# Two more Strassen blocks per MLP, squares moved to the scalar engine, and one address remainder for the matmul operands: a two-layer decoder trunk on one Trainium2 core

## The chip, the core and the metric

The kernel runs on one core of one Trainium2 chip. A core has four compute engines that run side by side, each with its own queue in program order: TensorE (PE in the profile; its loads of the stationary operand are shown apart as PEld), VectorE (DVE), ScalarE (ACT) and GpSimd (POOL). SyncE (SP) issues nearly all DMAs. The metric is device time of one launch in microseconds (us). Lower is better.

## The reference

A sequence of 256 tokens of width 1024 goes through two layers in float32. Each layer is an attention block and an MLP with squared ReLU:

```
def sqrelu_mlp(x, w1, w2):
    h = jax.nn.relu(x @ w1)
    return (h * h) @ w2

def reference(x, ...):
    h = x
    for layer in range(2):
        hn = rms_norm(h, norm_gain[layer, 0])
        h = h + (stick_breaking_attention(hn, ...) if layer == 0 else nsa_attention(hn, ..., shared))
        h = h + sqrelu_mlp(rms_norm(h, norm_gain[layer, 1]), mlp_w1[layer], mlp_w2[layer])
        if layer == 0:
            shared = nsa_shared_kv(h, kv_norm, ...)
    return rms_norm(h, final_norm)
```

`mlp_w1` is 1024 x 4096 and `mlp_w2` is 4096 x 1024. The change concerns the two MLPs, the transposes that lead into them, and one small product in the second layer's query projection.

## The kernel before

**Products in two parts.** Every large float32 product is made of three fast ones. An operand a is cut into a high part (rounded to the matmul's float32 form, fp32r) and a low part (a minus high). Then a.b is high.high + high.low + low.high. `mm3` issues these three. For weights, the high part is a cast on ACT (`cast`, L356, tile `wh`), the low part a subtraction on DVE (L371, tile `wl`), both from a 128 x 1024 tile `raw` that a DMA fills. There are six buffers each of `raw`, `wh` and `wl`.

**The MLP** (`mlp`, called once per layer) runs over 16 blocks of 256 hidden units. For block c, `first` multiplies the transposed normalised stream `xn` by two column halves of w1, 16 matmuls of 512 columns and 16 of 256 in all, into the PSUM tiles `pu`. ACT copies these to SBUF (`mu`, L630). `square` adds the two halves of `mu` (L645), takes relu and square in one DVE instruction (L646), cuts the result `ms` into `hh` (ACT, L650) and `hl` (DVE, L651), and makes the sums and differences of its 128 x 128 blocks that the second product wants (L659 to L662). `half(c, ., 0)` and `half(c, ., 1)` then multiply by the two halves of w2 into the PSUM tiles `acc`. Block c's `half` stands two blocks later in PE's queue: the loop over c issues `first(c)` and then the halves of block c - 2.

**Plain and fast blocks.** A block's second product is a 2 x 2 product of 128-row blocks (two halves of tokens, two halves of hidden units) with 512 columns of output each. A plain block takes 8 products, so 24 matmuls of 128 x 512 columns. The blocks listed in `FAST` use Strassen's scheme, 7 products and 21 matmuls. They need sums of w2's tiles (`sums`: `ty`, L384, L389, L390), and these sums cut into `th` and `tl` (L356, L397; four buffers each) besides the weights as they are. `FAST` before is blocks 2, 4, 6, 8, 10, 12 in both layers.

**What sets the order.** PE's order is the order of the Python code. The order on ACT, DVE and POOL is set while the program is built, by a planner (`Order`): each small operation is put with a rank and a cost in ns for each engine that may do it, and an engine that is free takes the ready operation of lowest rank. `o.quiet("D", ns)` keeps DVE from work of rank 2 or more for that time. Weights have rank 0.5 when PE needs them next, 2 or 4 when later.

**The start of an MLP.** `xt_turn` transposes the stream on PE (tiles `pt`), and `xt_evac` takes each transposed tile into `xn`: the high part on ACT (L504), the low part on DVE (L505). Half of the tiles is turned before the MLP, half inside it, after `first` of block 0's first half.

**The query projection of layer 1.** `q_proj` makes rotated queries of one of four head groups g: ACT copies to `qu` (L1233), DVE multiplies (`qm`, L1234) and shuffles (`qw`, L1236), then a product by a table (`qw`, L1237) and a sum (`qm`, L1240) that the planner may give to POOL or DVE.

**Addresses.** An SBUF tile's address within a partition is set when the program is built. The tiles `raw`, `wh`, `wl`, `xn`, `oT`, `xk` and `xq` all start at 160 bytes past a multiple of 256. The MLP's own pool starts at byte 156192, so `ms`, `hh`, `hl`, `th` and `tl` start at 32 past a multiple of 256.

Of the kernel before, what the change touches and what calls it, by code (L numbers as in the profile page):

```python
# [8 lines left out]
F32 = mybir.dt.float32  # L9
F32R = mybir.dt.float32r  # L10
BF16 = mybir.dt.bfloat16
AF = mybir.ActivationFunctionType
OP = mybir.AluOpType
AX = mybir.AxisListType

P = 128
D = 1024
# [7 lines left out]
DFF = 4096  # L25
NFC = 16
NGN = 6
FAST = ((2, 4, 6, 8, 10, 12),) * 2
EPS = 1e-5
NEG = -1e30  # L30
GELU_C = 2.0 * 0.7978845608028654
# [127 lines left out]
def act(n, f, more=0):  # L159
    return {"A": (195 + 0.835 * n + more, f, False)}  # L160


def dve(n, f, more=0, port=False):
    return {"D": (150 + 1.045 * n + more, f, port)}
# [7 lines left out]
def hybrid_kernel(ctx, tc, x, xt, eye, gcols, gfin, wqk, wv, wo0, wkv, wvs, wq, wg, wo1, w1, w2, cw1, cw2, cpos, gate_b, consts, out):  # L172
    nc = tc.nc
# [7 lines left out]
    o = Order()  # L181

    def go(gen, rank=1, lag=LAG):
        return Chain(o, gen, rank, o.now + lag)
# [3 lines left out]
    def f32(a):  # L188
        return a.bitcast(F32)

    def slot(i, shape, dt, name):
        return cp.tile(shape, dt, tag=f"e{i}", name=name, bufs=1)
# [4 lines left out]
    def B(i, name, dt=F32):  # L197
        return ps.tile([P, 512], dt, tag=f"b{i}", name=name, bufs=1)
# [7 lines left out]
    def feed(src, n, kind="w", parts=1, cuts=1, own=False, only=None):  # L206
        loads.append((src, n, cuts, own))
        return item(kind, only or n, [len(loads) - 1], parts)
# [14 lines left out]
    def feed_mlp(layer):  # L223
# [6 lines left out]
        def two(c, wide):  # L230
            s = [w2[layer, c][:, h * H:(h + 1) * H] for h in range(2)]
            fast = c in FAST[layer]
            x = feed(s[0], H)
# [180 lines left out]
    def W(i, part=None):  # L414
        if i > ws.cur:
            ws.cur = i
            for q in range(i, min(i + 4, len(items))):
                for c in ws.parts[q] or ():
                    c.hurry(rank_of(q))
        while any(ws.parts[q] is None for q in range(i + 1)):  # L420
            o.run(o.run(o.t))
        for p in range(items[i][3]) if part is None else (part,):
            for q in range(items[i][4] + p + 1):
                c = ws.parts[home[q]][q - items[home[q]][4]]
                if not c.done:
                    c.hurry()
            o.need(ws.parts[i][p])
        return ws.raws[items[i][2][0]] if items[i][0] == "r" else ws.made[i]

    def gone(x):  # L430
        for i in x if isinstance(x, list) else [x]:
            assert ws.gone == i, (ws.gone, i)
            ws.gone += 1
            if items[i][0] == "r":
                used(items[i][2][0])
        now, ws.waiting = ws.waiting, []
        for w in now:
            o.at(o.now, w.finish)
# [15 lines left out]
    def tr(o_, a, i, rate=2.0):  # L454
        nc.tensor.transpose(o_, a, i)  # L455
        o.tick(a.shape[0] / 2.4 * rate + 3)
# [39 lines left out]
    def xt_banks(banks):  # L496
        return [B(banks[b], f"pt{b}").rearrange("p (j q) -> p j q", j=2) for b in range(2)]

    def xt_evac(pt, j, b, half, gi, xt_, rank=0.5):
        k = 4 * half + 2 * b + j  # L500
        g = gc[:, gi * NK + k:gi * NK + k + 1]

        def one():
            yield act(256, lambda: nc.scalar.activation(xt_[0][:, k, :], pt[b][:, j, :], AF.Copy, scale=g), 60)  # L504
            yield dve(256, lambda: nc.vector.scalar_tensor_tensor(  # L505
                xt_[1][:, k, :], pt[b][:, j, :], g, f32(xt_[0][:, k, :]), op0=OP.mult, op1=OP.subtract), 60)
        return go(one(), rank)

    def xt_turn(pt, half, gi, xt_):
        ch = []  # L510
        for b in range(2):
            for j in range(2):
                k = 4 * half + 2 * b + j
                for t in range(T):
                    tr(pt[b][:, j, t * P:(t + 1) * P], hres[t][:, k * P:(k + 1) * P], ident)
            ch += [xt_evac(pt, j, b, half, gi, xt_) for j in range(2)]
        return ch
# [35 lines left out]
    def mlp(layer, gi, x_, ch, pt, rs, pus, accs, extra, mid, order, ends, ap):  # L553

        ws.tp = ap
        mus = slot(1, [P, 2, 2, 512], F32, "mu")
        mu = [mus[:, i] for i in range(2)]
        wa, wb = i_m[layer]
        fast = FAST[layer]
        acc = {}  # L560
# [40 lines left out]
        def begin(c):  # L601
            return ([B(pus[c % 2][f], f"pu{f}") for f in range(2)] if c < 4 else [None, None],
                    (mu[c % 2], ap.tile([P, 9, P], F32, name="ms")), [])
# [30 lines left out]
        def square(c, st):  # L634
            u, s = st[1]
            hh = ap.tile([P, 8 * P], F32R, name="hh", bufs=3)
            hl = ap.tile([P, 8 * P], F32R, name="hl", bufs=3)
            u4 = u.rearrange("p f (a q) -> p f a q", a=2)
            s4 = s[:, 0:4].rearrange("p (f t) q -> p f (t q)", f=2)
            flat = s.rearrange("p b q -> p (b q)")  # L640

            def gen():
                for x in st[2]:
                    yield x
                yield dve(512, lambda: nc.vector.tensor_add(s4, u4[:, :, 0], u4[:, :, 1]), port=True)  # L645
                yield dve(512, lambda: nc.vector.scalar_tensor_tensor(s4, s4, 0.0, s4, op0=OP.max, op1=OP.mult), port=True)  # L646

            def parts(a, b, at):
                q, into = slice(a * P, b * P), slice(at * P, (at + b - a) * P)
                yield act((b - a) * P, lambda: nc.scalar.copy(hh[:, into], flat[:, q]))  # L650
                yield dve((b - a) * P, lambda: nc.vector.tensor_sub(hl[:, into], flat[:, q], f32(hh[:, into])), port=True)  # L651

            def plain(g):
                yield g
                yield from parts(0, 4, 0)

            def mixed(g):
                yield g
                yield dve(256, lambda: nc.vector.tensor_sub(s[:, 4:6], s[:, 2::-2], s[:, 3:0:-2]), port=True)  # L659
                if c in fast:  # L660
                    yield dve(256, lambda: nc.vector.tensor_sub(s[:, 6:8], s[:, 1:5:3], s[:, 3:6:2]), port=True)
                    yield dve(128, lambda: nc.vector.tensor_sub(s[:, 8], s[:, 6], s[:, 0]), port=True)  # L662
                    yield from parts(5, 9, 4)
                else:
                    yield from parts(4, 6, 4)

            g = go(gen(), 0.4)
            at = {a: a for a in range(4)}
            at.update({S3: 4, S1: 5, S4: 6, S2: 7} if c in fast else {E2: 4, S3: 5})
            return hh, hl, (go(plain(g), 0.4), go(mixed(g), 0.41)), at  # L670
# [3 lines left out]
            first(0, st[0], f, 0, NK // 2)  # L674
        gone(wa[0][0])
        o.need(*rs)
        ch.extend(xt_turn(pt, 1, gi, x_))
        st.append(begin(1))
        for f in range(2):
# [315 lines left out]
    def layer1(xk, pt0, ch, ap):  # L995
# [215 lines left out]
        def q_proj(g, b, k0=0, k1=NK):  # L1211
            if k0 == 0:
                qps[g] = B(b, "qp")
            qp = qps[g]
            for k in range(k0, k1):
                w = W(i_q[g][k // 4])
                for j in range(2):
                    c = k % 4 * 256 + j * P
                    o.need(qc[k])
                    mm3(qp[:, j * 256:(j + 1) * 256], cut(w, c, c + P), both(xq, k), j == 0 and k == 0, k == NK - 1)  # L1220
                if k % 4 == 3:
                    gone(i_q[g][k // 4])
            if k1 < NK:
                return

            def gen():
                u = ap.tile([P, 2, T * P], F32, name="qu", bufs=3)
                m = ap.tile([P, 2, T * P], F32, name="qm", bufs=3)
                s = ap.tile([P, 2, T * P], F32, name="qw")
                src = qp.rearrange("p (j q) -> p j q", j=2)  # L1230
                tab = [rbc_[:, i, None, :].to_broadcast([P, 2, T * P]) for i in range(2)]
                yield rbc
                yield [act(512, lambda: nc.scalar.copy(u, src), -35),  # L1233
                       dve(512, lambda: nc.vector.tensor_mul(m, src, tab[0]))]  # L1234
                qu[g] = u
                yield dve(512, lambda: nc.vector.stream_shuffle(s, u, swap), 50)  # L1236
                yield {"G": (1040, lambda: nc.gpsimd.tensor_mul(s, s, tab[1]), True),  # L1237
                       "D": (690, lambda: nc.vector.tensor_mul(s, s, tab[1]), True)}
                yield {"G": (1260, lambda: nc.gpsimd.tensor_add(m, m, s), True),
                       "D": (690, lambda: nc.vector.tensor_add(m, m, s), True)}  # L1240
                qs[g] = m
            qch[g] = go(gen(), 0.8)

        qps, pvs = {}, {}
# [322 lines left out]
        pt = xt_banks((6, 7))  # L1567
# [14 lines left out]
    x1, ch, pt, rs = scoped(layer0, "l0")  # L1582
# [13 lines left out]
    x1, ch, pt, rs = scoped(layer1, "l1", nxt["x"], nxt["pt"], nxt["ch"], bufs=1)  # L1596
# [153 lines left out]
```

## Time and profile before

| | |
|---|---|
| median of 3 runs | 616.29 us (615.42 to 616.64) |
| the profiled execution, own time | 616.42 us |
| its span, first to last instruction | 614.6 us |
| mean granted TensorE clock | 0.997 |
| PE busy | 604.0 us (98%) |
| DVE busy | 507.2 us (83%) |
| ACT busy | 377.1 us (61%) |
| POOL busy | 40.6 us (7%) |

The profiled execution is 0.13 us above the median, and 1.8 us of it lie outside the span. The first MLP runs on PE from about 115 to 291 us of the span, the second from about 431 to 606 us. Busy PE time is a union of matmul records that overlap each other, so it doesn't tell how fast the matmuls follow one another. For that one reads the chain of waits, whose pieces lie end to end: a piece of so many matmuls, divided by their number, is the spacing from one to the next.

### The profile page before, as it was taken

Reading aid. Unit: us, or ns where it says so; the run is one execution under the profiler, and the core shown is the slowest. Engines: PE = TensorE matmul, PEld = TensorE weight load, DVE = VectorE, ACT = ScalarE, POOL = GpSimd, SP = SyncE. Lnnn points to the kernel's source line nnn. Section 1 sums busy time; section 2 is a strip of 40 time slices with the busy share of each in tenths; the row PEclk is TensorE's granted clock in tenths of the full one; section 3 lists DMA queues with packets and bytes.
Section 4 is the critical chain, followed back from the end, with each engine's and each line's share of the span. In section 5 each row is a group of like instructions: output and inputs, shape, how many; then the busy total and the mean of one; then the engine's idle time right before and its main releaser. Section 6 shows DMA issues by size and latency. Waiting matters only on the chain.

```text
span 614.6 us, 9427 instructions
## 1 busy us (share of the span) xinstructions
PE 604.0 (98%) x3544; PEld 507.7 (83%) x3544; DVE 507.2 (83%) x743; ACT 377.1 (61%) x623; POOL 40.6 (7%) x57
## 2 busy tenths in 40 slices
PE   8999999999999999999999999999999999999994
PEld 5899988888888888888887888677888888888884
DVE  6669996699889888986837999673997988988885
ACT  6757665566666566664806876462866756656642
POOL 0000000000000000000112442310000000000000
PEclk9999999999999999999999999999999999999998
DMA  8984444274574666565556544223656456465501
GB/s 313 394 275 138 138 134 137 75 262 158 179 245 148 210 203 191 186 231 170 173 170 206 174 145 163 69 70 103 213 164 228 149 193 235 155 209 202 172 0 70
DMA packets 31582, 108.30 MB, mean 176 GB/s; under 512 B 3888, under 2 KB 5168, under 8 KB 31536
## 3 DMA queue, kind: packets, MB, share of 16 engines
q1 hardware_dynamic: 30960, 107.07, 52.2%
q8 instruction: 28, 0.46, 0.3%
q10 hardware_dynamic: 576, 0.62, 0.3%
q14 instruction: 18, 0.15, 0.1%
HBM read 106.63 MB, written 1.05 MB: 175 GB/s over the span
## 4 chain that ended last, share of the span: by engine, by line
PE 90%; DVE 5%; DMA 2%; ACT 1%; issue 1%; POOL 0%; SPq 0%; POOLq 0%; ACTq 0%; DVEq 0%
PE acc L443 35%; PE pu L443 29%; PE qk L443 8%; PE pk L443 4%; PE pv L443 3%; PE po L443 3%; PE z L443 2%; PE qp L443 2%; DVE wl L371 2%; PE ph L443 1%; DMA raw<-in_wq 1%; PE pt L455 1%; PE pa L455 1%; DMA rv<-in_wv 1%; PE ptp L455 1%
## 5 line engine op out<-in xcount | busy, mean ns | idle before, releaser
L371 DVE TENSOR_TENSOR wl<-raw,wh 128x1024 fp32r<-128x1024 f32 (+1 forms) x180 | 210.0, 1190 | 30.9 <-ACT wh L356 29.4
L356 ACT CAST wh<-raw 128x1024 fp32r<-128x1024 f32 (+1 forms) x180 | 180.2, 1025 | 63.5 <-issue 23.2
L443 PE MATMUL pu<-xn,wh 128*128 128x512 f32 x512 | 129.8, 392 | 0.0
L443 PEld LDWEIGHTS pu<-xn,wh 128*128 128x128 f32 x512 | 94.8, 188 | 20.1 <-issue 0.5
L443 PE MATMUL acc<-wh,hl 128*128 128x512 f32 x196 | 77.1, 394 | 0.0
L443 PE MATMUL acc<-wh,hh 128*128 128x512 f32 x196 | 76.9, 393 | 0.0
L443 PE MATMUL acc<-wl,hh 128*128 128x512 f32 x196 | 76.9, 392 | 0.0
L443 PEld LDWEIGHTS pu<-xn,wl 128*128 128x128 f32 x512 | 70.8, 190 | 5.8
L443 PE MATMUL pu<-xn,wl 128*128 128x256 f32 x512 | 72.6, 282 | 0.0
L630 ACT COPY mu<-pu 128x512 f32<-128x512 f32 x64 | 37.3, 583 | 20.8 <-PE pu L443 20.8
L443 PE MATMUL qk<-xa,wh 128*128 128x256 f32 x256 | 47.3, 286 | 0.0
L650 ACT CAST hh<-ms 128x512 fp32r<-128x512 f32 x64 | 34.1, 553 | 16.4 <-DVE ms L646 12.9
L443 PE MATMUL acc<-wh,oT 128*128 128x512 f32 x128 | 43.6, 402 | 0.5 <-DVE oT L533 0.5
L443 PEld LDWEIGHTS acc<-wh,hl 128*128 128x128 f32 x196 | 36.8, 188 | 8.4
L443 PEld LDWEIGHTS acc<-wh,hh 128*128 128x128 f32 x196 | 37.1, 189 | 6.3
L443 PEld LDWEIGHTS acc<-wl,hh 128*128 128x128 f32 x196 | 36.9, 188 | 6.3
L356 ACT CAST th<-ty 128x1024 fp32r<-128x1024 f32 x24 | 25.2, 1051 | 26.2 <-DVE ty L390 13.8
L443 PEld LDWEIGHTS qk<-xa,wh 128*128 128x128 f32 x256 | 39.8, 192 | 0.5 <-issue 0.3
L651 DVE TENSOR_TENSOR hl<-ms,hh 128x512 fp32r<-128x512 f32 x64 | 37.3, 600 | 0.2 <-ACT hh L650 0.2
L443 PE MATMUL qk<-xa,wl 128*128 128x256 f32 x128 | 36.2, 283 | 0.0
L1276 ACT ACTIVATE pe<-z,nm 128x256 f32<-128x256 f32 (+1 forms) x64 | 26.3, 430 | 13.4 <-DVE nm L1282 10.2
L443 PE MATMUL pk<-wh,xk 128*128 128x512 f32 (+1 forms) x128 | 33.6, 342 | 0.0
(202 smaller groups left out, 949.2 us busy)
## 6 DMA issues: line engine op xcount, KB each, us to landing
raw<-in_w SPq DMA_DIRECT2D x128, 512.0 KB, 4.8
raw<-in_wqk SPq DMA_DIRECT2D x16, 512.0 KB, 5.8
raw<-in_wo SPq DMA_DIRECT2D x16, 512.0 KB, 4.2
raw<-in_wkv SPq DMA_DIRECT2D x8, 512.0 KB, 4.8
raw<-in_cw SPq DMA_DIRECT2D x8, 512.0 KB, 4.5
raw<-in_wq SPq DMA_DIRECT2D x8, 512.0 KB, 6.0
rv<-in_wv SPq DMA_DIRECT2D x6, 512.0 KB, 6.9
raw<-in_wvs SPq DMA_DIRECT2D x4, 512.0 KB, 5.7
```

The costliest lines, as they stand in the source:

```text
L356: k = {"A": (195 + 0.835 * m, lambda: nc.scalar.copy(a, b), False), "D": (200 + 0.49 * m, lambda: nc.vector.tensor_copy(a, b), True)}
L371: yield {"D": (150 + 1.045 * m, lambda: nc.vector.tensor_sub(lo, raw, f32(hi)), True)}
L443: nc.tensor.matmul(o_, a, b, start=first, stop=last, skip_group_check=True)
L455: nc.tensor.transpose(o_, a, i)
L630: yield act(512, lambda: nc.scalar.copy(u[:, f, :], pu[f]))
L650: yield act((b - a) * P, lambda: nc.scalar.copy(hh[:, into], flat[:, q]))
L651: yield dve((b - a) * P, lambda: nc.vector.tensor_sub(hl[:, into], flat[:, q], f32(hh[:, into])), port=True)
L1276: return act(n, lambda: nc.scalar.activation(d, z, AF.Exp, bias=nm[:, i:i + 1], accum_out=rs[:, t, hd, b:b + 1]), 150)
```

## The change

- `FAST` names eight blocks instead of six in each layer: 2, 3, 5, 6, 8, 9, 11, 12. In each layer two blocks turn from plain to fast, and pairs of fast blocks now follow each other.
- The one DVE instruction for relu and square of a block's 128 x 512 activations becomes two ACT instructions, `Relu` and `Square`.
- A tile of 128 bytes per partition (`pad`), used by nobody, is put first into the MLP's pool. `ms`, `hh`, `hl`, `th` and `tl` move from 32 to 160 past a multiple of 256 bytes, which is the remainder of the other matmul operands.
- `xt_evac` has rank 0.3 instead of 0.5, and DVE takes no work of rank 2 or more for 2200 ns after the attention's residual at the start of an MLP.
- In the query projection's last group (g = 3) the product by the table is made on DVE only.

```
-FAST = ((2, 4, 6, 8, 10, 12),) * 2
+FAST = ((2, 3, 5, 6, 8, 9, 11, 12),) * 2
...
-    def xt_evac(pt, j, b, half, gi, xt_, rank=0.5):
+    def xt_evac(pt, j, b, half, gi, xt_, rank=0.3):
...
     def mlp(layer, gi, x_, ch, pt, rs, pus, accs, extra, mid, order, ends, ap):
 
         ws.tp = ap
+        ap.tile([P, 32], F32, name="pad", bufs=1)
...
                 yield dve(512, lambda: nc.vector.tensor_add(s4, u4[:, :, 0], u4[:, :, 1]), port=True)
-                yield dve(512, lambda: nc.vector.scalar_tensor_tensor(s4, s4, 0.0, s4, op0=OP.max, op1=OP.mult), port=True)
+                yield act(512, lambda: nc.scalar.activation(s4, s4, AF.Relu))
+                yield act(512, lambda: nc.scalar.activation(s4, s4, AF.Square))
...
         gone(wa[0][0])
         o.need(*rs)
+        o.quiet("D", 2200)
         ch.extend(xt_turn(pt, 1, gi, x_))
...
-                yield {"G": (1040, lambda: nc.gpsimd.tensor_mul(s, s, tab[1]), True),
-                       "D": (690, lambda: nc.vector.tensor_mul(s, s, tab[1]), True)}
+                turned = {"G": (1040, lambda: nc.gpsimd.tensor_mul(s, s, tab[1]), True),
+                          "D": (690, lambda: nc.vector.tensor_mul(s, s, tab[1]), True)}
+                yield turned if g < 3 else {"D": turned["D"]}
```

Over the whole program PE issues 12 matmuls of 512 columns fewer. ACT issues 64 instructions more for relu and square, and DVE 32 fewer. Line numbers in the changed kernel are 1 to 4 higher from `mlp` on.

The order of the small operations is moved at three places that matter below. The first is DVE's queue at the start of the second MLP, from the residual `hres` on. Before:

```order
L539 TENSOR_TENSOR hres_72<-acc_4302,hres_72 128x512
L539 TENSOR_TENSOR hres_73<-acc_4303,hres_73 128x512
L371 TENSOR_TENSOR wl<-raw,wh 128x1024 x4
L505 SCALAR_TENSOR_TENSOR xn<-pt_4447,gc,xn 128x256 x2
L505 SCALAR_TENSOR_TENSOR xn<-pt_4448,gc,xn 128x256 x2
L371 TENSOR_TENSOR wl<-raw,wh 128x1024 x3
```

After:

```order
L539 TENSOR_TENSOR hres_72<-acc_4341,hres_72 128x512
L539 TENSOR_TENSOR hres_73<-acc_4342,hres_73 128x512
L371 TENSOR_TENSOR wl<-raw,wh 128x1024 x2
L505 SCALAR_TENSOR_TENSOR xn<-pt_4486,gc,xn 128x256 x2
L505 SCALAR_TENSOR_TENSOR xn<-pt_4487,gc,xn 128x256 x2
L371 TENSOR_TENSOR wl<-raw,wh 128x1024 x4
```

Two subtractions instead of four stand ahead of the low parts of `xn`. At the start of the first MLP it is two instead of three.

The second is ACT's queue in the first MLP, from the second copy of `pu` to the first `hh`. Before:

```order
L630 COPY mu<-pu_1273 128x512
L630 COPY mu<-pu_1316 128x512
L356 CAST wh<-raw 128x1024
L630 COPY mu<-pu_1317 128x512
L650 CAST hh<-ms 128x512
```

After:

```order
L631 COPY mu<-pu_1274 128x512
L631 COPY mu<-pu_1316 128x512
L356 CAST wh<-raw 128x1024
L631 COPY mu<-pu_1317 128x512
L647 ACTIVATE ms<-ms 128x512
L648 ACTIVATE ms<-ms 128x512
L356 CAST wh<-raw 128x1024
L631 COPY mu<-pu_1407 128x512
L652 CAST hh<-ms 128x512
```

Relu, square, one more weight cast and the first copy of block 2 (`pu_1407`) now stand ahead of the first `hh`.

The third is DVE's queue in the query projection of group 3, layer 1. Before:

```order
L1234 TENSOR_TENSOR qm<-qp,rbc 128x512
L371 TENSOR_TENSOR wl<-raw,wh 128x1024
L1236 STREAM_SHUFFLE qw<-qu 128x512
L371 TENSOR_TENSOR wl<-raw,wh 128x1024
L1240 TENSOR_TENSOR qm<-qm,qw 128x512
L533 TENSOR_TENSOR oT<-po,oT 128x512
```

After:

```order
L1237 TENSOR_TENSOR qm<-qp,rbc 128x512
L371 TENSOR_TENSOR wl<-raw,wh 128x1024
L1239 STREAM_SHUFFLE qw<-qu 128x512
L371 TENSOR_TENSOR wl<-raw,wh 128x1024
L1241 TENSOR_TENSOR qw<-qw,rbc 128x512
L1244 TENSOR_TENSOR qm<-qm,qw 128x512
L533 TENSOR_TENSOR oT<-po,oT 128x512
```

The product by the table has come from POOL into this queue, between the second subtraction and the sum.

## The prediction

> **What bounds the kernel now.** I read the page first, then PE's waits, busy time by stage, and the chain of waits for how closely the matmuls follow each other.
>
> ```profile
> PE 604.0 (98%) x3544; PEld 507.7 (83%) x3544; DVE 507.2 (83%) x743; ACT 377.1 (61%) x623; POOL 40.6 (7%) x57
> PE 90%; DVE 5%; DMA 2%; ACT 1%; issue 1%; POOL 0%; SPq 0%; POOLq 0%; ACTq 0%; DVEq 0%
> ```
>
> PE is busy for 98% of the span and makes 90% of the chain that ended last. This is only a hint, since matmul records overlap. The view of PE's waits says it better:
>
> ```profile
> PE pv L443 <- ACT wh L356: 1.0, 1, 1.0
> PE warm L443 <- PEq L1740: 0.8, 1, 0.8
> PE acc L443 <- DVE oT L533: 0.5, 1, 0.5
> PE ptp L455 <- DVE pT L1329: 0.3, 1, 0.3
> ```
>
> These four waits are all that PE has beyond its own pipeline, 2.6 us, and none lies in an MLP. So in the MLPs only two things count: how many matmuls PE has, and the spacing between them. Two stretches inside the MLPs, by windows (busy time of PE, PEld, DVE, ACT; then clock, DMA share, GB/s):
>
> ```profile
> 155.00:263.00 108.00, 108.00 (x548) 91.67 (x547) 96.33 (x131) 70.69 (x95) 0.00 (x0) 1.00 0.58 192
> 471.00:579.00 108.00, 108.00 (x548) 91.68 (x547) 95.88 (x131) 70.67 (x95) 0.00 (x0) 1.00 0.58 192
> ```
>
> DVE works 96.3 of 108 us (89%), ACT 65%, the clock is whole. DVE is the engine that could take PE's place. Now the spacing, from the chain of waits (start, length, what; the pieces lie end to end):
>
> ```profile
> 138.80 5.59 PE pu L443 x32
> ...
> 230.59 2.77 PE pu L443 x16
> 233.36 2.77 PE acc L443 x12
> 236.13 2.77 PE pu L443 x16
> 238.90 2.79 PE acc L443 x12
> 241.68 2.81 PE pu L443 x16
> 244.49 2.09 PE acc L443 x9
> ...
> 273.68 13.93 PE acc L443 x60
> ...
> 294.87 13.65 PE pk L443 x60
> ```
>
> The last two rows are the same 60 products, 128 x 512 fp32r, weights moving and activations stationary. `acc` in the MLP takes 232.2 ns each, `pk` in the key projection 227.5. The stationary operand of `acc` (`hh`, `hl`) starts at 32 past a multiple of 256 bytes while its moving weights start at 160. Both operands of `pk` start at 160. The `pu` rows, all of whose operands start at 160, take 2.77 in one place and 2.81 in another. The 2.81 comes right after `acc` products with `th` and `tl`, so a disturbed spacing lasts for some matmuls.
>
> **Fewer matmuls.** Four blocks lose one product of three matmuls: 12 at 232 ns from the row of 60, 2.8 us. All of it is on the path, since PE never waits there.
>
> **One address remainder.** The changed program still has 714 `acc` matmuls of 512 columns in the MLPs (174 x 3 with the weights, 64 x 3 with their sums). If they follow like `pk`, each saves 232.2 - 227.5 = 4.7 ns: 3.3 us. The disturbed `pu` rows go back to 2.77: 0.04 for each of the 12 fast blocks of before, and 5.59 against 2 x 2.77, 0.05, once in each layer: 0.6 us together. No row of before has `hh` at another address. So the bounds are 0, if the address isn't the cause, and 5, if every `acc` gets 227 ns (3.7) and `pu` gains twice as much as I see (1.2). A loss I leave out, as the new layout is the one in which `pk` runs already. I take 3.9, by the `pk` row, which differs from `acc` in nothing else that I can name.
>
> The Trainium skill speaks against this term. "SBUF — State Buffer", section "Who interferes with whom", gives PE two independent read ports, one for the moving operand and one for the stationary, and says that PE waits for nobody; "Operand start alignment" there treats a start address as a matter of legality. By that page the pad is worth nothing and my sum would be 3.9 us poorer; the rows of 13.93 and 13.65 us do not fit a spacing that is free of the operands' place, but show no address by themselves.
>
> **The start of the MLPs.** In the timeline of the second start (start, length, engine, operation):
>
> ```profile
> 431.24 1.07 PE L443 MATMUL pu<-xn,wh 128*128 128x512 f32 x4
> 432.61 4.62 DVE L371 TENSOR_TENSOR wl<-raw,wh 128x1024 fp32r<-128x1024 f32 x4
> 434.66 1.57 ACT L504 ACTIVATE xn<-pt,gc 128x256 fp32r<-128x256 f32 x4 [0.34 <-PE pt L455]
> 434.82 1.19 PE L443 MATMUL pu<-xn,wh 128*128 128x512 f32 x4
> 437.15 1.65 DVE L505 SCALAR_TENSOR_TENSOR xn<-pt,gc,xn 128x256 fp32r<-128x256 f32 x4
> 437.71 1.71 PE L443 MATMUL pu<-xn,wh 128*128 128x512 f32 x4
> ```
>
> Four matmuls of `pu` take 1.07 when nothing disturbs them. At 437.71 they take 1.71, since the low parts of `xn` come one by one from 437.15 on, behind four subtractions. With two ahead DVE is free 2.3 us earlier, at 434.9, and ACT's first tile is there at 435.1. The four low parts then end by 436.8, before 437.7, and 0.64 us go, with 0.11 of the 1.19. I count 0.75 here and nothing at the first start, where one subtraction of three goes. Bounds 0 and 0.9. The subtractions put off are for later weights. Behind them DVE idles 11% of the MLP, so they are caught up.
>
> **Relu and square on ACT.** Durations by form (count, busy, mean ns):
>
> ```profile
> L371 DVE TENSOR_TENSOR wl<-raw,wh 128x1024 fp32r<-128x1024 f32 x168 | 201.8, 1226 | 30.9 <-ACT wh L356 29.4 <-PE pv L443 1.3
> L651 DVE TENSOR_TENSOR hl<-ms,hh 128x512 fp32r<-128x512 f32 x44 | 30.0, 683 | 0.2 <-ACT hh L650 0.2
> L397 DVE TENSOR_TENSOR tl<-ty,th 128x1024 fp32r<-128x1024 f32 x24 | 29.3, 1220 | 1.0 <-ACT th L356 0.4
> L646 DVE SCALAR_TENSOR_TENSOR ms<-ms 128x512 f32<-128x512 f32 x32 | 21.9, 685 | 0.1
> L384 DVE TENSOR_TENSOR ty<-raw 128x1024 f32<-128x1024 f32 x12 | 14.6, 1221 | 0.0
> L659 DVE TENSOR_TENSOR ms<-ms 128x256 f32<-128x256 f32 x32 | 13.4, 420 | 0.4
> L650 ACT CAST hh<-ms 128x512 fp32r<-128x512 f32 x44 | 27.3, 620 | 16.2 <-DVE ms L646 12.9 <-DVE ms L662 3.3
> L356 ACT CAST th<-ty 128x1024 fp32r<-128x1024 f32 x24 | 25.2, 1051 | 26.2 <-DVE ty L390 13.8 <-DVE ty L384 12.4
> ```
>
> For a first reckoning take 0.68 us for every DVE operation of 512 columns and 0.42 for 256 (0.28 for 128). A plain block costs DVE 4 x 1.226 for its weights, then sum 0.68, square 0.685, `hl` 0.68 + 0.42 and a difference 0.42: 7.8. A fast block costs 3 x 1.226 + 0.68 for weights, 2 x 1.220 for `tl`, 1.221 + 2 x 0.68 for `ty`, then 0.68 + 0.685 + 2 x 0.683 + 2 x 0.42 + 0.28: 13.2. Five pairs make 105, against 96.3 busy, since neighbours overlap: a factor of 0.91. A pair is now 19.1 us of DVE on 21.5 of PE (230.59 to 252.12 in the chain). Afterwards the square is gone, 7.1 and 12.5. Fast, fast and plain come to 32.1 x 0.91 = 29.2 us. PE needs for them 3 x 5.54 for `pu` and 66 x 227.5 ns: 31.6. So DVE goes from 89% to 92%, still under PE. Over a whole layer its work stays about equal: 16 x 0.685 saved, 2 x 5.4 added. ACT gains two operations a block that I price like `hh`, 0.62 each (between 0.55, as they overlap, and the 1.05 of 1024 columns): per three blocks 3.7 more, and 1.0 for half a fast block in place of half a plain one, on 21.2 (three halves of 70.7 / 5): 26 of 31.6. I count nothing. What hides it is the lead of two blocks; if it went, the next late thing would be `hh`.
>
> The place where the lead is least is the first block of the first MLP:
>
> ```profile
> 130.15 0.68 DVE L651 TENSOR_TENSOR hl<-ms,hh 128x512 fp32r<-128x512 f32 x1
> 130.53 0.59 ACT L630 COPY mu<-pu 128x512 f32<-128x512 f32 x1
> ...
> 133.22 5.58 PE acc L443 x24
> ```
>
> `hl` is done at 130.8, and the first `acc` starts at 133.2 (last row: the chain). After the change `hh` stands behind the copy of block 2, which can't end before 131.1, so `hh` ends at 131.7 and `hl` at 132.4. That leaves 0.8 us or a little more. Cost 0, bound 1 us.
>
> **The table product of group 3.**
>
> ```profile
> 383.76 1.21 DVE L371 TENSOR_TENSOR wl<-raw,wh 128x1024 fp32r<-128x1024 f32 x1
> 383.95 2.15 POOL L1237 TENSOR_TENSOR qw<-qw,rbc 128x512 f32<-128x512 f32 x1 [3.58 <-DVE qw L1236]
> 386.13 0.69 DVE L1240 TENSOR_TENSOR qm<-qm,qw 128x512 f32<-128x512 f32 x1 [1.16 <-POOL qw L1237]
> 386.74 0.68 DVE L533 TENSOR_TENSOR oT<-po,oT 128x512 fp32r<-128x512 f32 x1
> 387.48 0.50 PE L443 MATMUL acc<-wh,oT 128*128 128x512 f32 x1 [0.54 <-DVE oT L533]
> ```
>
> DVE stands idle 1.16 us for POOL's 2.15, and `oT` behind it keeps PE waiting 0.54. On DVE the product (0.69 like L1240) starts at about 384.9 and the queue is 0.5 to 0.6 earlier from there on. PE gets back 0.5. Bounds 0 and 0.7.
>
> **The sum.** 2.8 + 3.9 + 0.75 + 0.5 = 7.95 us. The profiled execution took 616.4, so 608.4; it stands 0.1 above the median, so 608.3 against the runs.
>
> **Rivals.**
> - *The remainder doesn't matter.* The pad does nothing; the 4.7 ns come from something else about `hh`, such as its place high in the memory. For it: the products of `th` with `hh`, both at 32, are as slow (9 in 2.09, 232 ns). Against it: those runs are six long, and a disturbance was seen to outlast eight. Time: 616.3 - 4.05 = 612.3. The skill's page named above would have it so.
> - *DVE becomes the bound* where two fast blocks follow each other. Two cost DVE 25.0 x 0.91 = 22.8 us against PE's 2 x 10.3 = 20.6. The 2.2 us must come from the lead, which the plain block restores (6.5 of DVE on 11.0 of PE). It decides if the lead is under 2.2 at a pair. The eight pairs then cost up to 18; with half the deficit at every pair, 8.8, it is 617, and with only the first pair of each layer late 612.7. DVE's 11% idle time speaks against it.
> - *Slower: the chain to `hh` gets late on ACT in every block.* Two operations of 0.62 in place of 0.685, with up to two casts of 1.05 in between, make the chain up to 2.7 us longer; the lead seen in the first block was 2.4. With 0.25 us too much in each of 32 blocks the gain is gone; at 0.4 it is 12.8 - 7.95: 621. Against it: only the first block has so little lead, the later ones have ACT idle a third of the time. By the Trainium skill, "ScalarE: Activation LUTs", "Rules for kernel authors", relu and multiplication belong on VectorE; 1.24 against 0.685 us agrees, and would push this way.
>
> **Chances.** The forecast 0.66, no gain by address 0.18, DVE too late 0.07, ACT too late 0.05, something else that eats it 0.04. The forecast's own range is 606.4 (every term at its best bound, 2.8 + 5 + 0.9 + 0.7 = 9.4, and half a microsecond for the unseen) to 610. The range goes to 612.6 to take in the second case, and leaves out some 0.17. Faster by over 0.2%, that is 1.2 us, about what the runs can tell: 0.66 + 0.18 and most of DVE's case, 0.90. Same 0.05, slower 0.05.
>
> **What would show it.** In the changed profile the chain should have `acc` pieces of 12 at 2.73 and `pu` pieces of 16 at 2.77 throughout, 12 `acc` matmuls fewer, no `pu` piece near 1.7 at the second start, and `acc` after the table product without `oT` as releaser. Pieces of `acc` at 2.77 to 2.79 would mean that the remainder isn't the cause. PE waiting for `hl`, `tl` or `wl` in the MLP would make the forecast wrong.

## The result, and the profile after

The changed kernel takes 609.39 us (median, 608.84 to 610.00). The kernel before, run beside it on the same chip, takes 616.15 (615.42 to 616.64). The ratio is 0.9892, with a 95% interval from 0.9874 to 0.9909: a gain of 6.8 us, where 8 were forecast. The profiled execution took 609.23 us, and its span is 607.1 us against 614.6.

The first page of the profile and the shares of the chain:

```profile
PE 598.2 (99%) x3532; PEld 505.5 (83%) x3532; DVE 511.0 (84%) x740; ACT 417.0 (69%) x695; POOL 38.6 (6%) x56
PE 92%; DVE 4%; issue 1%; ACT 1%; DMA 1%; SPq 0%; POOLq 0%; POOL 0%; DVEq 0%
```

PE has its 12 matmuls fewer (3532 after 3544). DVE did not get lighter: its 16 x 0.685 us of squares in each layer went to ACT, and two more fast blocks took their place. ACT has 40 us more. The view of PE's waits is now this, whole:

```profile
PE warm L443 <- PEq L1744: 0.8, 1, 0.8
PE pv L443 <- ACT wh L356: 0.2, 1, 0.2
```

The wait for `oT` is gone. PE is as full as before, so what was won lies in how many matmuls there are and how closely they follow. Busy time in the same two stretches of the MLPs (PE, PEld, DVE, ACT, POOL; clock, DMA share, GB/s):

```profile
155.00:263.00 108.00, 108.00 (x556) 92.49 (x555) 100.51 (x134) 84.61 (x119) 0.00 (x0) 1.00 0.60 196
471.00:579.00 108.00, 108.00 (x551) 92.33 (x550) 100.57 (x133) 87.02 (x123) 0.00 (x0) 1.00 0.60 197
```

DVE is at 93% (forecast 92), ACT at 78 and 81% (forecast 82). The chain of waits gives the spacing (start, length, what):

```profile
138.27 5.56 PE pu L443 x32
...
189.29 2.07 PE acc L443 x9
191.36 2.77 PE pu L443 x16
...
204.47 2.75 PE acc L443 x12
207.22 2.77 PE pu L443 x16
...
270.70 13.63 PE acc L443 x60
...
291.57 13.65 PE pk L443 x60
...
582.94 13.64 PE acc L443 x60
```

The 60 products of `acc` now take what those of `pk` take: 13.63 and 13.64 us after 13.93. Runs of 9 went from 2.09 to 2.07, runs of 12 from 2.77 or 2.79 to 2.75, and `pu` is at 2.77 in 44 of the 46 pieces of 16, without a 2.81.

The program can be cut at four places by the starts of PE's instructions: the first `pu` of each MLP, the first `pk`, and the last matmul. The table has these lengths in us, worked out from the traces, for all kernels of this study. "Second start" is the part of the second MLP from its first `pu` to its first `acc` with `hh`.

| kernel | layer 0 attention | first MLP | second attention | second MLP | of it second start |
|---|---|---|---|---|---|
| before | 115.40 | 175.71 | 140.14 | 175.35 | 18.27 |
| after | 114.97 | 172.85 | 139.38 | 171.88 | 17.68 |
| pad_only | 114.90 | 174.21 | 139.88 | 173.83 | 18.26 |
| fast_only | 114.31 | 174.46 | 139.91 | 174.10 | 18.26 |
| no_pad | 115.03 | 174.46 | 139.35 | 173.51 | 17.68 |
| square_on_dve | 114.36 | 172.95 | 139.78 | 171.88 | 17.68 |
| pads_64_192 | 115.12 | 173.75 | 139.74 | 173.62 | 17.67 |
| pads_256_384 | 114.24 | 174.46 | 139.39 | 171.88 | 17.68 |
| all_at_32 | 114.96 | 172.81 | 139.69 | 173.49 | 17.65 |
| no_quiet | 114.61 | 172.85 | 139.36 | 172.46 | 18.25 |
| rank_and_table | 114.76 | 172.85 | 140.05 | 171.88 | 17.68 |
| ten_fast | 114.48 | 185.66 | 139.56 | 185.68 | 17.68 |
| nine_fast | 114.15 | 172.29 | 139.39 | 171.19 | 17.67 |

The MLPs repeat to a tenth of a microsecond between kernels that have the same matmuls and addresses there, the two attention stages only to half a microsecond or more. So the small terms are read here from the stages and not from whole times. Of the 7.58 us between the two spans, 6.33 lie in the MLPs (2.86 and 3.47), 0.76 in the second attention and 0.43 in the first, in which the change does nothing: DVE, ACT and POOL have the same order there in both traces.

### The profile page after: what moved, and what is told of

It reads as the page before. It is cut to its first block, busy times and chain, and to the rows that moved or that the text cites. A ratio compares the mean times of both kernels' runs of the same rounds, so it can differ in the third digit from the quotient of the medians.

```text
span 607.1 us, 9410 instructions
## 1 busy us (share of the span) xinstructions
PE 598.2 (99%) x3532; PEld 505.5 (83%) x3532; DVE 511.0 (84%) x740; ACT 417.0 (69%) x695; POOL 38.6 (6%) x56
## 4 chain that ended last, share of the span: by engine, by line
PE 92%; DVE 4%; issue 1%; ACT 1%; DMA 1%; SPq 0%; POOLq 0%; POOL 0%; DVEq 0%
PE acc L443 34%; PE pu L443 29%; PE qk L443 8%; PE pk L443 4%; PE pv L443 3%; PE po L443 3%; PE qp L443 3%; PE z L443 3%; DVE wl L371 1%; PE ptp L455 1%; PE ph L443 1%; PE pt L455 1%; PE pa L455 1%; DVE nm L1286 1%; DMA rv<-in_wv 1%
## 5 line engine op out<-in xcount | busy, mean ns | idle before, releaser
L356 ACT CAST wh<-raw 128x1024 fp32r<-128x1024 f32 (+1 forms) x180 | 177.4, 1015 | 27.0 <-PE qk L443 9.4
L443 PE MATMUL pu<-xn,wh 128*128 128x512 f32 x512 | 128.5, 390 | 0.0
L443 PE MATMUL acc<-wh,hh 128*128 128x512 f32 (+1 forms) x176 | 68.9, 391 | 0.0
L443 PE MATMUL acc<-wl,hh 128*128 128x512 f32 (+1 forms) x176 | 68.8, 391 | 0.0
L443 PE MATMUL acc<-wh,hl 128*128 128x512 f32 (+1 forms) x176 | 68.3, 388 | 0.0
L397 DVE TENSOR_TENSOR tl<-ty,th 128x1024 fp32r<-128x1024 f32 x32 | 39.1, 1222 | 6.5 <-ACT th L356 6.5
L443 PEld LDWEIGHTS acc<-wh,hl 128*128 128x128 f32 x176 | 33.1, 188 | 7.1
L443 PEld LDWEIGHTS acc<-wh,hh 128*128 128x128 f32 x176 | 33.3, 189 | 5.2
L443 PEld LDWEIGHTS acc<-wl,hh 128*128 128x128 f32 x176 | 33.3, 189 | 4.9
L356 ACT CAST th<-ty 128x1024 fp32r<-128x1024 f32 x32 | 33.6, 1051 | 4.8 <-DVE ty L384 3.9
L1280 ACT ACTIVATE pe<-z,nm 128x256 f32<-128x256 f32 (+1 forms) x64 | 26.2, 429 | 12.9 <-DVE nm L1286 12.8
```

The source lines that it names most:

```text
L356: k = {"A": (195 + 0.835 * m, lambda: nc.scalar.copy(a, b), False), "D": (200 + 0.49 * m, lambda: nc.vector.tensor_copy(a, b), True)}
L397: yield {"D": (150 + 1.045 * H, lambda: nc.vector.tensor_sub(lo, ty, f32(hi)), True)}
L443: nc.tensor.matmul(o_, a, b, start=first, stop=last, skip_group_check=True)
L1280: return act(n, lambda: nc.scalar.activation(d, z, AF.Exp, bias=nm[:, i:i + 1], accum_out=rs[:, t, hd, b:b + 1]), 150)
```

## The experiments

**Each half of the main gain alone.** Theory: the gain is the matmul count and one remainder for all operands. Rivals: the pad does nothing; or DVE is the bound. Four kernels ran together, beside a median before of 615.91 us.

*pad_only* is the kernel before with one line of the change:

```
     def mlp(layer, gi, x_, ch, ...):
         ws.tp = ap
+        ap.tile([P, 32], F32, name="pad", bufs=1)
```

> The kernel before with the pad alone, so that all operands of the MLPs' matmuls start at 160 past a multiple of 256 bytes. Theory (matmuls lock to 227 ns each only where all operands share the remainder): the 738 acc matmuls of 512 columns of this kernel come some 3 to 4 ns closer, 2.3 to 3.4 us, and pu after a fast block's acc loses its 0.04 us each time, 0.5 in all: 2.5 to 4 us faster than before, 612.2 to 613.7; acc x12 in the chain of waits at 2.75 or less. Rival (the remainder doesn't matter; the closer spacing of the changed kernel comes from its order): no difference, 616.2, and acc x12 stays at 2.77 to 2.79.

Measured: 612.84 us, ratio 0.995 (0.9937 to 0.9962), 3.1 us faster. From its chain of waits:

```profile
151.99 2.75 PE acc L443 x12
154.74 2.77 PE pu L443 x16
157.50 2.07 PE acc L443 x9
...
272.00 13.63 PE acc L443 x60
```

The 128 bytes alone give the close spacing. All four engines have the same instructions in the same order as before, so the order has no part in it. The MLPs are 1.50 and 1.52 us shorter, 3.0 together. The expectation counts 738 `acc` matmuls of 512 columns; the trace has 726. The rival that the remainder doesn't matter is out.

*no_pad* is the changed kernel without that line.

> The changed kernel without the pad: hh, hl, th, tl again at 32 past a multiple of 256, the weights at 160. Theory (equal remainders): acc x12 back to 2.78, acc x60 back to 13.9, pu after acc of a fast block back to 2.81: 2.5 to 3.5 us longer than the changed kernel, 612 to 613. Rival (order, not remainder): same as the changed kernel, 609.4.

Measured: 612.63 us, ratio to before 0.9947 (0.9934 to 0.9961), 3.2 above the changed kernel. The spacing of before is back:

```profile
219.16 2.81 PE pu L443 x16
221.96 2.09 PE acc L443 x9
224.06 2.77 PE pu L443 x16
226.82 2.79 PE acc L443 x12
...
272.06 13.93 PE acc L443 x60
```

*fast_only* is the kernel before with eight fast blocks:

```
-FAST = ((2, 4, 6, 8, 10, 12),) * 2
+FAST = ((2, 3, 5, 6, 8, 9, 11, 12),) * 2
```

> The kernel before with eight fast blocks in each layer and nothing else: square on DVE in one operation, operands at the old places. Theory (matmul count, PE never waits): 12 matmuls fewer at 232 ns, 2.8 us faster, 613.4, and DVE, which keeps the square, goes to some 94% in two fast blocks and a plain one without PE waiting for it. Rival (DVE is the bound where fast blocks adjoin, and only the square's move to ACT makes room): PE waits for tl, wl or hl in the MLPs; with half a microsecond at each of the eight pairs the gain is 4 us smaller, 617 or more.

Measured: 613.88 us (612.56 to 614.23), ratio 0.9961 (0.9949 to 0.9974), between 1.6 and 3.1 us faster. By the table the MLPs lose 1.25 us each, 2.50. Of this 2.7 are matmuls that are gone; 0.2 come back, since four more runs of 12 end with the disturbed `th` and `tl` products, and the `pu` behind each takes 2.80 or 2.81. No wait in an MLP appears, though DVE still has the square and is at 97%, where 94 were expected (window row as above):

```profile
155.00:263.00 108.00, 108.00 (x549) 91.70 (x548) 104.46 (x142) 73.59 (x98) 0.00 (x0) 1.00 0.59 192
```

*square_on_dve* is the changed kernel with the old operation:

```
-                yield act(512, lambda: nc.scalar.activation(s4, s4, AF.Relu))
-                yield act(512, lambda: nc.scalar.activation(s4, s4, AF.Square))
+                yield dve(512, lambda: nc.vector.scalar_tensor_tensor(s4, s4, 0.0, s4, op0=OP.max, op1=OP.mult), port=True)
```

> The changed kernel with relu and square as one DVE operation again (512 columns, 0.685 us, 32 times) in place of two on ACT. Theory (the MLPs are bound by matmul count and spacing, and both engines have room): the same time as the changed kernel within 0.5 us, 609 to 610, DVE's busy time up by some 20 us and ACT's down by some 40. Rival (DVE is the bound where fast blocks adjoin): PE gets waits for wl, tl or hl in the MLPs, and the time is 1 to 5 us longer, 610.5 to 614.

Measured: 609.28 us, ratio 0.9892 (0.9879 to 0.9906), the changed kernel's own. DVE works 105.6 of 108 us, and PE waits for nothing in the MLPs:

```profile
155.00:263.00 108.00, 108.00 (x556) 92.55 (x554) 105.55 (x143) 74.59 (x99) 0.00 (x0) 1.00 0.59 195
```

By the table the first MLP is 0.1 us longer than in the changed kernel and the second the same. So the move to ACT gives next to nothing at eight fast blocks, and a DVE busy for 98% of a stretch is not yet the bound.

**Which remainder.** Three kernels, each with a different layout in each MLP, tell whether it is equality, the value 160, or any shift. Each ran once, and they are compared by the lengths of their MLPs. The weights are at 160 past a multiple of 256 in the first two.

*pads_64_192* has `ap.tile([P, (16, 48)[layer]], ...)` as its pad, so `hh` to `tl` are at 96 in the first MLP and at 224 in the second.

> The changed kernel with a pad of 64 bytes in the first MLP and of 192 in the second: hh, hl, th, tl start at 96 past a multiple of 256 in the first and at 224 in the second, the weights at 160 as ever. Read from the trace: the spacing of the acc matmuls in each MLP and the length of each (172.9 and 171.9 us in the changed kernel, 175.7 and 175.4 before). Theory by remainders of 256: neither is equal, so both MLPs are as slow as with 32: acc x12 at 2.77 to 2.79, 2.5 to 3 us longer in each, 615. Theory by remainders of 64 (all of 96, 224 and 160 are 32 past a multiple of 64): as the changed kernel, 609.4. Theory that only 32 is bad: as the changed kernel.

Measured: 612.64 us. The first MLP is 0.90 longer than in the changed kernel, the second 1.74. From the chain, one run of 60 in each:

```profile
271.66 13.73 PE acc L443 x60
...
585.74 14.02 PE acc L443 x60
```

Remainders of 64 are out. None of the three theories had both sizes: 64 below the weights costs about half of what 128 away does, 64 above costs slightly more. The cost does not lie in the same place either. With 64 below, the short runs of `acc` are as close as in the changed kernel, and the `pu` behind them are slow, though both of their own operands stay at 160:

```profile
205.05 2.75 PE acc L443 x12
207.80 2.79 PE pu L443 x16
```

Summed from start to start and set against the changed kernel, 64 below costs 0.25 us in `acc` and 0.66 in `pu`, and 64 above 1.41 in `acc` and 0.33 in `pu`. So it is the stream of matmuls that loses its close spacing, not each unequal pair by itself.

*pads_256_384* has `(64, 96)[layer]`: 32 past a multiple of 256 again in the first MLP, but with a pad, and 160 in the second, 256 bytes higher than in the changed kernel.

> The changed kernel with a pad of 256 bytes in the first MLP and of 384 in the second. In the first, hh to tl start at 32 past a multiple of 256 again, as before, but 256 bytes higher; in the second at 160 past a multiple of 256 and 256 bytes higher than in the changed kernel. Theory by remainders of 256: the first MLP is 1.3 to 1.7 us longer than in the changed kernel, with acc x12 at 2.77 to 2.79, and the second as in the changed kernel, with acc x12 at 2.75: 611. Theory that room or height in the memory counts, or any shift: both alike.

Measured: 610.09 us. The first MLP is 1.61 longer, the second is the changed kernel's to 0.01:

```profile
271.26 13.93 PE acc L443 x60
...
583.83 13.64 PE acc L443 x60
```

So the period is 256 bytes: 64, 128 and 192 move the time, another 256 does not. A pad as such does nothing.

*all_at_32* moves the weights instead:

```
+    cp.tile([P, 32], F32, name="shift")
...
-        ap.tile([P, 32], F32, name="pad", bufs=1)
+        if layer == 0:
+            ap.tile([P, 32], F32, name="pad", bufs=1)
```

> The changed kernel with 128 bytes more ahead of the long-lived tiles, so that the weights, xn and ty start at 32 past a multiple of 256 instead of 160; no pad in the first MLP, so that hh to tl are at 32 there too, and the pad in the second, which puts hh to tl at 160 there. Theory that equality counts: the first MLP stays as in the changed kernel (all at 32; acc x12 at 2.75), and the second is 1.3 to 1.7 us longer (32 against 160; acc x12 at 2.78). Theory that 160 is a good remainder for hh and 32 a bad one: the other way round, the first longer and the second as in the changed kernel.

The expectation names the pad the wrong way round. The tile `shift` stands ahead of the weights' rings and of `xn` and moves what lies above them as well, so it is the first MLP that keeps the pad and the second that has none. The addresses are as it says.

Measured: 611.36 us. The first MLP, all of it at 32, takes 172.81 us (changed kernel 172.85). The second, with `hh` at 160 and the weights at 32, takes 173.49, 1.61 longer:

```profile
270.67 13.63 PE acc L443 x60
...
584.47 13.95 PE acc L443 x60
```

Equality it is, at 32 as at 160; 160 has no merit of its own.

**The small edits.** Undone on the changed kernel, in two kernels that each ran once.

*no_quiet* leaves out `o.quiet("D", 2200)`.

> The changed kernel without the quiet stretch of 2200 ns on DVE at the start of each MLP; the rank of 0.3 for the evacuations of xn stays. Theory (the subtractions ahead of xn's low parts were the delay, and quiet holds them back): the second start, from the first pu to the first acc with hh, takes 18.27 us again as in the kernel before, instead of 17.68, and one pu piece of four lasts 1.7. Rival (the rank alone puts the evacuations first): it stays at 17.68.

Measured: 609.16 us, and the second start is 18.25 again, so the edit is worth 0.57. The late `pu` is back in the timeline:

```profile
433.29 1.69 PE L443 MATMUL pu<-xn,wh 128*128 128x512 f32 x4
```

*rank_and_table* sets the rank of the evacuations to 0.5 and lets POOL take the product of group 3:

```
-    def xt_evac(pt, j, b, half, gi, xt_, rank=0.3):
+    def xt_evac(pt, j, b, half, gi, xt_, rank=0.5):
...
-                yield turned if g < 3 else {"D": turned["D"]}
+                yield turned
```

> The changed kernel with the rank of xn's evacuations at 0.5 again and the table product of group 3 free to go to POOL. In the order of the instructions the rank then changes nothing, and only the product moves, from DVE back to POOL. Theory: PE waits 0.5 us for oT after it again (the gap ahead of that acc 0.7 to 0.8 us instead of 0.28), and the second MLP starts as in the changed kernel, 17.68. Rival (the wait was for something else): the gap stays at 0.28.

Measured: 609.40 us. The rank moves no instruction: ACT and PE have the changed kernel's order, and DVE and POOL differ by the one product. The product is back on POOL, and with it the wait, from the timeline of the second layer's queries:

```profile
380.35 2.15 POOL L1240 TENSOR_TENSOR qw<-qw,rbc 128x512 f32<-128x512 f32 x1 [3.56 <-DVE qw L1239]
382.54 0.69 DVE L1244 TENSOR_TENSOR qm<-qm,qw 128x512 f32<-128x512 f32 x1 [1.16 <-POOL qw L1240]
383.15 0.68 DVE L533 TENSOR_TENSOR oT<-po,oT 128x512 fp32r<-128x512 f32 x1
...
383.89 0.50 PE L443 MATMUL acc<-wh,oT 128*128 128x512 f32 x1 [0.56 <-DVE oT L533]
```

From the start of the `ptp` transpose ahead of it to that `acc` there are 836 ns here, 280 in the changed kernel: 0.56 us.

**How many fast blocks.** *ten_fast* has blocks 2 to 6 and 8 to 12 fast.

> The changed kernel with ten fast blocks in each layer instead of eight (2 to 6 and 8 to 12): four blocks more, each with one product of three matmuls less, 12 x 228 ns = 2.7 us. Theory (matmul count while DVE keeps its lead): 606.7. Rival (DVE too late): five fast blocks in a row cost DVE 12.5 x 0.91 = 11.4 us each by the prediction's figures against PE's 10.3, 5.5 us behind by the end of the five, more than a lead of about two blocks' operands may hold: PE waits for wl or tl, and the time is 608 to 615.

Measured: 634.58 us, ratio 1.0299 (1.0285 to 1.0313), 25 us slower than the changed kernel for 12 matmuls less. Neither expectation has this; the rival went up to 615. PE's three longest waits:

```profile
PE acc L443 <- DVE tl L397: 14.1, 20, 0.8
PE acc L443 <- DVE wl L371: 1.8, 2, 1.6
PE acc L443 <- DVE hl L653: 1.3, 1, 1.3
```

From the timeline, inside a run of fast blocks (start, length, engine; in brackets the idle time before it and what ended it):

```profile
233.10 1.05 ACT L356 CAST th<-ty 128x1024 fp32r<-128x1024 f32 x1 [2.75 <-DVE ty L390]
...
234.18 1.22 DVE L397 TENSOR_TENSOR tl<-ty,th 128x1024 fp32r<-128x1024 f32 x1 [1.11 <-ACT th L356]
...
235.46 0.50 PE L443 MATMUL acc<-tl,hh 128*128 128x512 f32 x1 [0.76 <-DVE tl L397]
```

The sum `ty` goes from DVE to ACT, comes back as `th`, and PE waits for the `tl` made from it. The cast `th` starts at 233.10, 246.00 and 258.91 in the chain: 12.9 us for a fast block, on 10.3 of PE. The three casts belong to the second run of five. DVE is busy for only 90% of these blocks, as of the larger stretch:

```profile
155.00:263.00 108.00, 101.91 (x504) 83.47 (x504) 97.61 (x133) 77.56 (x110) 0.00 (x0) 1.00 0.51 168
```

Yet DVE's queue sets this pace. From 246.00 to 258.91 it works 11.66 us, and once in each block it stands idle for 1.11 us, between the sum `ty` and the `tl` that waits for ACT's cast of that sum. Work and this wait make 12.8 of the 12.9. It isn't for want of buffers: no idle time of DVE or ACT there ends with a matmul.

Whether PE feels it depends on the lead, the time from the end of `tl` to its product. Worked out from the traces for the two halves of each fast block among blocks 2 to 9 of the first MLP, in us:

```
after      10.5 8.7 |  8.8 8.3 | plain     |  9.4 7.5 |  7.0 5.3 | plain     | 11.1 8.9 |  8.1 6.2
ten_fast   10.5 8.7 |  8.8 8.3 |  5.0 2.7  |  1.0 0.1 |  0.1 0.1 | plain     |  4.1 1.8 |  0.8 0.1
nine_fast  10.5 8.7 |  8.8 8.3 |  5.0 2.7  | plain    |  7.7 5.7 |  5.8 4.7  |  4.7 2.4 | plain
```

Second halves are compared with second halves here, as the first half of a block has more lead. In the changed kernel the second block of a pair takes 2.2 us (7.5 to 5.3) and 2.7 us (8.9 to 6.2). In ten_fast the third fast block in a row brings the lead from 8.3 to 2.7, the fourth to 0.1, and from there to the end of the run PE waits in every half. Behind a plain block the lead is up to 3.6 us higher again (5.3 to 8.9). So a run of two or three can be paid for and one of five can't. Why the third block takes 5.6 us, more than the 2.6 by which 12.9 exceeds 10.3, is not worked out here.

*nine_fast* has three runs of three: `FAST = ((2, 3, 4, 6, 7, 8, 10, 11, 12),) * 2`.

> The changed kernel with nine fast blocks in each layer in runs of three (2 to 4, 6 to 8, 10 to 12) instead of eight in pairs: 6 matmuls fewer, 1.36 us. In the trace of the changed kernel tl is ready 8.7 us ahead of its product in the first fast block, 5.3 us at the end of a pair, and 11 us again after a plain block. With ten blocks, of which five adjoin, the lead went 8.7, 8.3, 2.7, 0.1 and then PE waited 2.5 us in every fast block. Theory that the lead of a plain block carries three: 608.0. Theory that the third fast block already costs more than a plain block gives back: PE waits for tl in the second and third run of three, some 2.5 us each in both layers, 609 to 618.

Measured: 607.65 us (606.79 to 608.05), ratio 0.987 (0.9854 to 0.9887), where the changed kernel has 0.9892. The two intervals overlap; the MLPs are 0.56 and 0.69 us shorter by the table, 1.25 of the 1.36 that six matmuls make. PE's only wait in the whole trace is at the program's start, and DVE works 102.6 us:

```profile
PE warm L443 <- PEq L1744: 0.8, 1, 0.8
```

```profile
155.00:263.00 108.00, 108.00 (x555) 92.49 (x554) 102.62 (x139) 86.73 (x120) 0.00 (x0) 1.00 0.58 193
```

So it beats the kernel before, and in the MLPs the changed kernel too; the whole times alone don't settle the second. Ten blocks in runs of five are too many. Runs of four, or ten fast blocks with the square on DVE, were not tried.

## Why the prediction was nearly right

The time came out 1.1 us above the forecast. Its terms, against what the stages measured:

| term | predicted | measured | by |
|---|---|---|---|
| fewer matmuls | 2.8 | 2.5 | fast_only, both MLPs |
| one remainder | 3.9 | 3.2 | changed kernel against no_pad, both MLPs (3.0 by pad_only) |
| second start | 0.75 | 0.57 to 0.59 | no_quiet, and the start before |
| table product | 0.5 | 0.56 | the gap in rank_and_table |
| Relu and Square on ACT | 0 | 0 | square_on_dve |
| sum | 7.95 | 6.9 | |

- *The remainder.* The mechanism is shown; the term was mis-sized. The step that failed is "If they follow like `pk`, each saves 4.7 ns". The rows of 60 keep that promise (13.93 to 13.63, 5 ns each), but most `acc` come in runs of 9 and 12 behind the 256-column products of `pu`, and the start of a run is slow in either layout. From start to start, in ns, the mean over the 14 runs of 12 behind `pu` in the first MLP:

```
place in the run    1   2   3   4   5   6   7   8   9  10  11  12   sum
no_pad            231 232 228 230 233 241 236 232 234 226 231 229  2782
after             234 236 228 232 231 227 227 227 227 227 227 227  2748
```

With equal remainders the spacing locks to 227 ns from the sixth on; without, it never does. A run of 12 saves 34 ns and not 56. Summed over both MLPs, `acc` gained 2.4 us instead of 3.3, and `pu` 0.8 instead of 0.6. The forecast "pieces of 12 at 2.73" is 2.75 for this reason. That the address was the cause was a choice by one row, with 0.18 left for the other case; the experiments settled it.

- *The rival that the remainder doesn't matter* had the Trainium skill on its side. The Trainium skill, "SBUF — State Buffer", section "Who interferes with whom", gives PE two independent read ports and no partner that it could wait for. Taken as saying that the operands' addresses don't count, it differs from the measurement, which decides: unequal remainders of 256 bytes cost 3.1 us, by pad_only, where nothing else changed.

- *Fewer matmuls.* 12 fewer at 232 ns was right for the matmuls (2.7 by their summed spacing in fast_only). With the pad the four blocks would be worth 12 x 229.

- *The start.* `xn`'s low parts now run from 431.49 to 433.15, and no `pu` of four is long:

```profile
431.49 1.66 DVE L505 SCALAR_TENSOR_TENSOR xn<-pt,gc,xn 128x256 fp32r<-128x256 f32 x4 [0.59 <-ACT xn L504]
...
433.07 4.62 DVE L371 TENSOR_TENSOR wl<-raw,wh 128x1024 fp32r<-128x1024 f32 x4
433.66 1.09 PE L443 MATMUL pu<-xn,wh 128*128 128x512 f32 x4
```

The 0.6 for the 1.71 came; the 0.11 in the 1.19 did not (it is 1.18 at 430.77). The quiet stretch does all of it, the rank nothing.

- *ACT and DVE.* The two operations on ACT take 0.63 each (0.62 assumed), both together nearly twice the 0.685 of DVE. The Trainium skill, "ScalarE: Activation LUTs", "Rules for kernel authors", puts relu and multiplication on VectorE; the durations agree, the time doesn't care, as square_on_dve shows. In the first block, the place of least lead, `hl` ends near 132.3 and its first product starts at 133.10, so 0.8 us are left. The forecast's 132.4 stands on the clock of the kernel before, whose first MLP begins 0.43 later: counted from the first `pu`, `hl` ends at 17.3 us, where 17.0 were forecast.

- *DVE as the bound at adjoining fast blocks.* The reckoning of 11.4 us of DVE for a fast block was close: in ten_fast it works 11.66. The reckoning left out the 1.11 us that DVE waits for `th`, which make it 12.8. What spoke against it in the prediction, "DVE's 11% idle time", was the weaker reason: at 2% idle square_on_dve loses 0.1 us, and at 10% idle ten_fast loses 25. The 2.2 us that a pair was to take from the lead are 2.2 and 2.7 here. The pairs are safe because the lead never falls under 5.3 us in the changed kernel.

## What to carry to other kernels

Where PE never waits, measure the spacing of its matmuls from start to start, run by run, and compare it with that of another stage of the same shape; if it is longer, look at the start addresses of all matmul operands of the stream modulo 256 bytes before anything else. Price such a gain by the run length that the kernel has: here the first five matmuls of each run did not take part. How much more work an engine ahead of PE can take is read from the lead of its last operand and how that falls and recovers from block to block, not from its busy share.

## What the hardware showed that was not expected

- A stream of matmuls (128 x 512, fp32r) in which all stationary and moving operands start at the same remainder of 256 bytes locks to 227 ns. With the stationary operands of `acc` 128 away, rows of 60 average 232 (13.93 us); with them 64 above, 234 (14.02); with them 64 below, 229 (13.73). The sign matters. Why, no run here tells.
- The slow spacing outlasts its cause: `pu`, all at 160, took 2.81 instead of 2.77 behind a run of 12 that ends with `th` and `tl`, and 2.79 or 2.80 where `hh` to `tl` lie 64 below the weights. The first five `acc` behind 256-column `pu` take 228 to 236 ns each with equal remainders too.
- DVE can be busy for 98% of a stretch of 108 us without PE ever waiting for it.
